# A branch by token count in the layer-0 experts: four column groups for at most 32 tokens, and another order behind the first product

## The chip, the cores and the metric

The kernel runs on one core of a Trainium2 chip. The metric is the device time of one execution in microseconds. Five engines work side by side, each on a queue of its own: TensorE (PE, its weight loads PEld), VectorE (DVE), ScalarE (ACT), GpSimd (POOL) and SyncE (SP, which only issues transfers). They wait for each other by semaphores.

## What is computed

A decoder trunk of two layers over 1024 tokens of width 1024, all in float32. Each layer has a mixer (pooling in layer 0, gated linear attention in layer 1) and a mixture of 64 experts in 8 groups. A token goes to one group and to two experts in it. The part that the change touches:

```python
group_sizes = jnp.bincount(flat_id, length=MOE_EXPERTS).astype(jnp.int32)
gu = lax.ragged_dot(xs, w_in, group_sizes)            # 1024 -> 2 x 384
gate, up = jnp.split(gu, 2, axis=-1)
ys = lax.ragged_dot(jax.nn.silu(gate) * up, w_out, group_sizes)   # 384 -> 1024
ys = ys * weights.reshape(-1)[order][:, None].astype(ys.dtype)
out = jnp.zeros_like(t).at[token_of].add(ys)
```

Each expert has 3 MB of `w_in` and 1.5 MB of `w_out`, and 2048 places for tokens are spread over 64 experts, 32 on average.

## The kernel before

**The experts.** `moe` (L608) walks the 64 experts of a layer in one unrolled loop. The tokens of an expert come in portions of 64, each token as two halves of 512 channels, so that a gathered tile has 128 rows (half, token). For expert e:

- `gather` (L501, POOL) fetches the rows of expert e + 2.
- `expert_first` (L530) multiplies: stationary are 64 tokens by 128 channels (`xT`), moving are 384 columns of `w_in`. The gate goes to one half of a PSUM bank's partitions, the up part to the other, eight steps of 128 channels, 16 `matmul` calls, each two instructions in float32.
- `expert_in` (L508) of expert e + 1 follows on TensorE: four transposes (L512). ScalarE (L520) and VectorE (L522) then scale and shift four pieces each.
- `expert_hidden` (L542): Silu of the gate on ScalarE (L545), times the up part on VectorE (L546).
- `expert_turn` (L548): three transposes (L554) and a copy on ScalarE (L555).
- `expert_last` (L557): the product with `w_out` (L563), weights and gate in `expert_add` (L567), and an accumulating scatter into `x_d` (L569).
- An `If` on the expert's count (L664) does a second portion of up to 64 tokens. The four engines with work in it load the count from `kept` (L619) and branch. TensorE's join waits until the work ahead of it is done.
- `load` issues the three transfers of expert e + 2 (L498, L499) from SyncE into the ring `RING0` of six slots; they stand behind that join, and wait for it.

**Which path.** In layer 1, and for experts 2 to 15 of layer 0, `expert_either` does the whole with one `If`/`Else`. Experts 0, 1 and 16 to 63 of layer 0 go through `expert_out` (L574). Groups are ordered by size, so that early experts have more tokens.

**The filler.** While the experts of layer 0 run, TensorE also computes the input projection of layer 1 in float16 halves. `prep_norm` and `prep_out` prepare a block of 128 tokens (a norm, transposes, two casts on ScalarE at L932); `piece` cuts its product into 49 units: one small product (L944), then 48 pieces of three matmuls (L957), and after each eight of these an eviction on ScalarE (L959) and a transfer to DRAM (L960). `expert_out` runs two units before the turn, two before `expert_last` and four after it, as long as there are units: eight experts have room for 64.

**Order.** TensorE's instructions in the loop stand as the code is written (`manual_schedule`). The other engines' order is made by the scheduler, within the blocks that branches bound. Engines run their queues in order.

Of the kernel before, what the change touches and what calls it, by code (L numbers as in the profile page):

```python
# [11 lines left out]
AF = mybir.ActivationFunctionType  # L12
OP = mybir.AluOpType
AX = mybir.AxisListType
ET = mybir.EngineType
# [4 lines left out]
NE = 64  # L20
# [16 lines left out]
def trunk_kernel(ctx, tc, x_in, c_in, norm_gain, w_mod, b_mod, pool_w, pool_b, pool_scale,  # L37
# [4 lines left out]
    V, S, T, G, SP = nc.vector, nc.scalar, nc.tensor, nc.gpsimd, nc.sync  # L42
# [6 lines left out]
    A = [slots.tile([128, 3072], F32, name=f"slot{i}") for i in range(16)]  # L49
# [7 lines left out]
    def part(slot, kb, n):  # L57
        a = int(kb * 256)
        return A[slot][:, a:a + n]

    def ps():
        return psum.tile([128, 512], F32, name="ps")
# [4 lines left out]
    def cv(n):  # L67
        taken[0] += n
        return kept[:, taken[0] - n:taken[0]]
# [3 lines left out]
    ident = cv(128)  # L73
# [12 lines left out]
    cnt_i = cv(88)[0:1, :].bitcast(I32)  # L86
    wz_, isc_ = cv(128), cv(128)
    wz = wz_.rearrange("p (a b) -> p a b", a=8)
    zst = part(15, 11.25, 32).rearrange("p (b f) -> p b f", b=2)
    ig = cv(128).rearrange("p (a b) -> p a b", a=2).bitcast(I32)  # L90
    isc = isc_.rearrange("p (a b) -> p a b", a=2).bitcast(I32)
    wsl = cv(128).rearrange("p (a b) -> p a b", a=2)
# [1 line left out]
    so = small[:, 58:66].bitcast(I32)  # L94
    G2 = cv(512)
    gs = part(15, 11.5, 40)
    gmax, ginv, gmul, gadd = (gs[:, 8 * i:8 * i + 8] for i in range(4))
    gout = gs[:, 32:33]
    gtmp = gs[:, 33:37]
# [30 lines left out]
    p = ps()  # L130
# [4 lines left out]
    p = ps()  # L135
# [145 lines left out]
    def as16(a):  # L281
        return a.bitcast(BF16)

    def route_consts(area):

        ones_b, trim = as16(area("ones", 64)), as16(area("trim", 64))
        V.memset(ones_b, 1.0)
        V.tensor_tensor(trim, slot_no, pno.to_broadcast([128, 128]), op=OP.is_le)
        V.tensor_scalar(trim, trim, -1.0, None, op0=OP.mult)
        return ones_b, trim  # L290
# [215 lines left out]
    mark = []  # L506
# [23 lines left out]
    def expert_first(i, sl, b=None):  # L530
        xT = part(15, 2 * i, 512).rearrange("p (c g t) -> p c g t", c=4, g=2)
        p1 = ps()
        n = 0
        for g in range(2):
            for cc in range(4):
                W = A[sl[g]].rearrange("p (k u f) -> p k u f", k=4, u=2)[:, cc]
                for u, s in enumerate(sides(i if b is None else b)):
                    T.matmul(p1[s, 0:384], xT[:, cc, g, :], W[:, u], start=n == 0, stop=n == 7)  # L538
                n += 1
        return p1  # L540

    def expert_hidden(b, p1):  # L542
        gate, up = sides(b)
        hh = part(15, 4, 384)[up]
        S.activation(hh, p1[gate, 0:384], AF.Silu)  # L545
        return V.tensor_tensor(hh, hh, p1[up, 0:384], op=OP.mult).ins  # L546

    def expert_turn(b):  # L548
        s = sides(b)[1]
        hh = part(15, 4, 384)[s].rearrange("p (r c) -> p r c", c=3)  # L550
        hT = part(15, 5.5 + 0.75 * b, 192)
        p3 = ps()
        for cc in range(3):
            T.transpose(p3[:, cc * 64:(cc + 1) * 64], hh[:, :, cc], ident[s, s])  # L554
        return S.copy(hT, p3[:, 0:192]).ins  # L555

    def expert_last(b, sl):  # L557
        hT = part(15, 5.5 + 0.75 * b, 192)
        o = A[sl[2]].rearrange("p (k f) -> p k f", k=3)
        p2 = ps()  # L560
        for cc in range(3):
            for g in range(2):
                T.matmul(p2[g * 64:g * 64 + 64, :], hT[:, cc * 64:(cc + 1) * 64],  # L563
                         o[:, cc, g * 512:(g + 1) * 512], start=cc == 0, stop=cc == 2)
        return p2

    def expert_add(l, p2, w, sidx, y):  # L567
        V.scalar_tensor_tensor(XG[y], p2, w, G2, op0=OP.mult, op1=OP.mult)  # L568
        ins = G.indirect_dma_start(out=yv[l], out_offset=bass.IndirectOffsetOnAxis(ap=sidx, axis=0), in_=XG[y],  # L569
                                   in_offset=None, bounds_check=2 * SEQ - 1, oob_is_err=False, compute_op=OP.add).ins  # L570
        while moved:
            tc.add_manual_dep(ins, moved.pop().name, DATA_SYNC, reason="it adds to what they wrote")

    def expert_out(l, i, sl, to, y, between=None, fill=lambda n: None):  # L574
        p1 = expert_first(i, sl)
        if between:
            between()
        fill(2)
        mark[:] = [expert_hidden(i, p1)]
        mark.append(expert_turn(i))  # L580
        fill(2)
        p2 = expert_last(i, sl)
        fill(4)
        expert_add(l, p2, *to, y)

    def expert_either(l, i, sl, to, y, nxt, many, to2, y2, aside):

        def hidden(b, p, n):
            if n:
                return expert_in(l, n[0], n[1], lambda: expert_hidden(b, p))  # L590
            return expert_hidden(b, p)

        p1 = expert_first(i, sl)
        with tc.If(many) as cmp:
            ins = hidden(i, p1, (i, y2))
            aside(ins, expert_turn(i))
            p2 = expert_last(i, sl)
            p1b = expert_first(i, sl, 1 - i)
            expert_add(l, p2, *to, y)
            hidden(1 - i, p1b, nxt)  # L600
            expert_turn(1 - i)
            expert_add(l, expert_last(1 - i, sl), *to2, y2)
        with cmp.Else():
            ins = hidden(i, p1, nxt)
            aside(ins, expert_turn(i))
            expert_add(l, expert_last(i, sl), *to, y)

    def moe(l, ring, mb, ob, load, ng, na, filler=None, before=None, aside=None, after=None):  # L608


        nr = len(ring)
        to = ig if l else isc
        pool_only = (ET.Pool,)

        def slots_at(e):
            return [ring[(3 * e + j) % nr] for j in range(3)]

        def count(e, engines):
            return nc.values_load(cnt_i[0:1, e:e + 1], engines=engines, min_val=0, max_val=SEQ,  # L619
                                  skip_runtime_bounds_check_because=COUNT_REASON)  # L620

        def main(e):
            return mb[e % len(mb)]

        def more(e):
            return ob[e % len(ob)]

        def ahead(e):
            if e < NE:
                with tc.If(count(e, pool_only) > 64):  # L630
                    gather(ig[:, 1, e:e + 1], more(e))

        for e in range(na):
            ahead(e)
        expert_in(l, 0, main(0))
        for e in range(NE):
            i = e % 2
            sl = slots_at(e)

            def between():  # L640
                if e + 1 < NE:
                    expert_in(l, 1 - i, main(e + 1))

            if before:
                before(e)
            if e + ng < NE:
                gather(ig[:, 0, e + ng:e + ng + 1], main(e + ng))
            tos = [(wsl[:, k, e:e + 1], to[:, k, e:e + 1]) for k in range(2)]
            engines = (ET.Pool, ET.Activation, ET.PE, ET.DVE)
            if l or 1 < e < NE // 4 and not units:  # L650
                ahead(e + na)
                expert_either(l, i, sl, tos[0], main(e), (1 - i, main(e + 1)) if e + 1 < NE else None,
                              count(e, engines) > 64, tos[1], more(e), aside or (lambda *marks: None))
                if after:
                    after(e)
            else:
                expert_out(l, i, sl, tos[0], main(e), between,
                           (lambda n: filler(e, n)) if filler else (lambda n: None))
                if aside:
                    aside(*mark)  # L660
                if after:
                    after(e)
                ahead(e + na)
                with tc.If(count(e, engines) > 64):  # L664
                    expert_in(l, i, more(e))
                    expert_out(l, i, sl, tos[1], more(e))
            for s in range(nr + 3 * e, min(nr + 3 * e + 3, 3 * NE)):
                load(s // 3, s % 3, slots_at(s // 3))
# [114 lines left out]
    for half in range(2):  # L783
        s = slice(half * 512, half * 512 + 512)
        S.copy(Q1[:, s], row_psum(pcol[:, 8:16], half, dg[0]))
        p = row_psum(pcol[:, 0:8], half, dg[1])
# [38 lines left out]
    def urgent(r):  # L825
        with tc.high_priority():
            next(r)
            next(r)
        next(r)

    urgent(route(0, 0, NT, area0, route_consts(area0)))
    gather(ig[:, 0, 0:1], 0)
    last = gather(ig[:, 0, 1:2], 1)
# [138 lines left out]
    def filler(e, n):  # L972
        if e < NE - 1:
            run_units(min(n, len(units) - 32) if e > NE - 6 else n)

    def aside(*marks):
        with tc.issue_after(marks[0]), tc.issue_after(marks[1]):
            for step in steps[:4]:
                step()
# [467 lines left out]
```

## Time and profile before

| | us |
|---|---|
| three runs | 2326.62, 2328.43, 2334.72 |
| median | 2328.43 |
| the profiled execution | 2327.7 |
| its span, first to last instruction | 2326.0 |
| TensorE busy in it | 1984.6 (85%) |
| VectorE, ScalarE, GpSimd busy | 718.9, 622.7, 496.9 |
| DMA | 770 MB, mean 331 GB/s |
| experts 16 to 63 of layer 0 | 426 to 1165 |
| layer 1's experts | 1495 to 2295 |

The granted TensorE clock was 0.964 of full speed in the mean. Busy shares of the whole are means over stages with different limits; what the changed stage waits for is read in that stage. In a timeline a row's idle time stands in brackets, with what ended it.

### The profile page before, as it was taken

Reading aid. Unit: us, or ns where it says so; the run is one execution under the profiler, and the core shown is the slowest. Engines: PE = TensorE matmul, PEld = TensorE weight load, DVE = VectorE, ACT = ScalarE, POOL = GpSimd, SP = SyncE. Lnnn points to the kernel's source line nnn. Section 1 sums busy time; section 2 is a strip of 40 time slices with the busy share of each in tenths; the row PEclk is TensorE's granted clock in tenths of the full one; section 3 lists DMA queues with packets and bytes.
Section 4 is the critical chain, followed back from the end, with each engine's and each line's share of the span. In section 5 each row is a group of like instructions: output and inputs, shape, how many; then the busy total and the mean of one; then the engine's idle time right before and its main releaser. Section 6 shows DMA issues by size and latency. Waiting matters only on the chain. (4 is left out here: it accounts for less than half of the span.)

```text
span 2326.0 us, 31279 instructions
## 1 busy us (share of the span) xinstructions
PE 1984.6 (85%) x11195; PEld 945.5 (41%) x11196; DVE 718.9 (31%) x1759; ACT 622.7 (27%) x1418; POOL 496.9 (21%) x422
## 2 busy tenths in 40 slices
PE   7968888899999999999888999888878777778784
PEld 5644333344444444444334565433323332333331
DVE  3454545211121121212147567422211111112122
ACT  4222323322222121212126665221211111112113
POOL 0303222122222221222124110222212212122210
PEclk9979999999999999999988999899999999999997
DMA  9979989998978999989945942699999999999995
GB/s 347 370 297 393 394 292 346 370 342 326 346 286 310 335 363 341 369 313 365 348 132 169 332 165 87 260 395 386 398 382 391 385 380 390 379 391 386 393 382 206
DMA packets 222566, 770.03 MB, mean 331 GB/s; under 512 B 31623, under 2 KB 41261, under 8 KB 201822
## 3 DMA queue, kind: packets, MB, share of 16 engines
q1 hardware_dynamic: 177074, 684.66, 75.4%
q0 software_dynamic: 43856, 77.67, 12.0%
q10 hardware_dynamic: 1372, 4.28, 0.5%
q8 instruction: 154, 2.52, 0.4%
q14 instruction: 110, 0.90, 0.1%
HBM read 735.44 MB, written 69.80 MB: 346 GB/s over the span
## 5 line engine op out<-in xcount | busy, mean ns | idle before, releaser
L538 PE MATMUL ps<-slot,slot 128*64 128x384 f32 x4416 | 757.5, 493 | 94.7 <-DMA slot<-in_moe_w_in_dram 76.2
L538 PEld LDWEIGHTS ps<-slot,slot 128*64 128x64 f32 x4416 | 336.2, 138 | 517.3 <-issue 247.7
L563 PE MATMUL ps<-slot,slot 128*64 128x512 f32 x1656 | 405.4, 626 | 48.0 <-ACT slot L555 46.2
L545 ACT ACTIVATE slot<-ps 64x384 f32<-64x384 f32 x138 | 67.0, 485 | 1265.1 <-PE ps L538 1236.1
L957 PE MATMUL ps<-slot,slot 128*128 128x512 f16 x1152 | 278.8, 388 | 8.6 <-DVEq L1094 5.7
L522 DVE TENSOR_SCALAR slot<-ps,kept 128x64 f32<-128x64 f32 x552 | 151.1, 334 | 339.8 <-PE ps L512 338.5
L546 DVE TENSOR_TENSOR slot<-slot,ps 64x384 f32<-64x384 f32 x138 | 75.8, 549 | 528.4 <-ACT slot L545 527.6
L569 POOL DMA_INDIRECT x_d<-kept x96 | 159.2, 1659 | 362.4 <-DVEq L664 172.1
L563 PEld LDWEIGHTS ps<-slot,slot 128*64 128x64 f32 x1656 | 110.9, 141 | 247.7 <-issue 184.2
L502 POOL DMA_INDIRECT kept<-h_d,kept x96 | 102.1, 1064 | 499.8 <-DMA x_d<-kept 296.6
L520 ACT ACTIVATE slot<-ps,kept 128x64 f32<-128x64 f32 x552 | 178.4, 403 | 59.3 <-PE ps L512 51.2
L568 DVE SCALAR_TENSOR_TENSOR kept<-ps,kept 128x512 f32<-128x512 f32 x96 | 72.0, 750 | 328.8 <-PE ps L563 325.9
L957 PEld LDWEIGHTS <-slot 128*128 128x128 f16 x1152 | 108.2, 100 | 156.3 <-issue 50.1
L554 PE MATMUL ps<-kept,slot 64*128 64x64 f32 x414 | 76.0, 291 | 91.7 <-DVE slot L546 91.4
L554 PEld LDWEIGHTS ps<-kept,slot 64*128 64x128 f32 x414 | 57.8, 202 | 135.7 <-DVE slot L546 102.3
L569 POOL DMA_INDIRECT x_d<-slot,kept x42 | 67.2, 1601 | 159.6 <-DVE slot L568 96.0
L502 POOL DMA_INDIRECT slot<-h_d,kept x42 | 44.2, 1053 | 230.3 <-DMA x_d<-slot,kept 91.5
L1269 PE MATMUL ps<-slot,slot 128*128 128x512 f16 x384 | 85.7, 379 | 1.2 <-DVE slot L1261 0.9
L568 DVE SCALAR_TENSOR_TENSOR slot<-ps,kept 128x512 f32<-128x512 f32 x42 | 31.5, 751 | 122.4 <-PE ps L563 116.5
L512 PE MATMUL ps<-kept 128*128 128x128 f32 x384 | 63.1, 287 | 2.4 <-DMA kept<-h_d,kept 2.4
L512 PEld LDWEIGHTS ps<-kept 128*128 128x128 f32 x384 | 40.4, 141 | 60.5 <-issue 57.1
L1269 PEld LDWEIGHTS <-slot 128*128 128x128 f16 x384 | 37.1, 98 | 46.7 <-issue 2.1
(336 smaller groups left out, 1672.6 us busy)
## 6 DMA issues: line engine op xcount, KB each, us to landing
slot<-in_moe_w_in_dram SPq DMA_DIRECT2D x256, 1536.0 KB, 12.4
slot<-in_moe_w_out_dram SPq DMA_DIRECT2D x128, 1536.0 KB, 13.0
slot<-in_w_mod_dram SPq DMA_DIRECT2D x24, 1536.0 KB, 11.8
slot<-in_gla_w_in_dram SPq DMA_DIRECT2D x8, 1536.0 KB, 8.2
slot<-in_w_mod_dram SPq DMA_DIRECT2D x8, 1152.0 KB, 6.7
h_d<-slot POOLq DMA_DIRECT2D x16, 512.0 KB, 7.1
slot<-in_x_dram SPq DMA_DIRECT2D x8, 512.0 KB, 11.6
slot<-x_d POOLq DMA_DIRECT2D x8, 512.0 KB, 7.2
```

What stands on the lines that cost most here:

```text
L502: return G.indirect_dma_start(out=XG[i], out_offset=None, in_=hv, in_offset=bass.IndirectOffsetOnAxis(ap=idx, axis=0), bounds_check=2 * SE ...
L512: T.transpose(pp[cc % 2][:, cc // 2 * 128:cc // 2 * 128 + 128], XG[g][:, cc * 128:(cc + 1) * 128], ident)
L520: S.activation(xT[:, cc, g, :], pv[:, g, :], AF.Identity, bias=sh, scale=sc)
L522: ins = V.tensor_scalar(xT[:, cc, g, :], pv[:, g, :], sc, sh, op0=OP.mult, op1=OP.add).ins
L538: T.matmul(p1[s, 0:384], xT[:, cc, g, :], W[:, u], start=n == 0, stop=n == 7)
L546: return V.tensor_tensor(hh, hh, p1[up, 0:384], op=OP.mult).ins
L554: T.transpose(p3[:, cc * 64:(cc + 1) * 64], hh[:, :, cc], ident[s, s])
L563: T.matmul(p2[g * 64:g * 64 + 64, :], hT[:, cc * 64:(cc + 1) * 64], o[:, cc, g * 512:(g + 1) * 512], start=cc == 0, stop=cc == 2)
L568: V.scalar_tensor_tensor(XG[y], p2, w, G2, op0=OP.mult, op1=OP.mult)
L569: ins = G.indirect_dma_start(out=yv[l], out_offset=bass.IndirectOffsetOnAxis(ap=sidx, axis=0), in_=XG[y], in_offset=None, bounds_check=2 * ...
L957: T.matmul(p, hP[:, m, kc, :], W[:, n, :], start=kc + i == 0, stop=kc == KC - 1 and i == 2)
L1269: T.matmul(p, oT[:, m, kc, :], woh[kc][:, n, half * 512:(half + 1) * 512], start=kc + i == 0, stop=kc == KC - 1 and i == 2)
```

## The change

Experts 0, 1 and 16 to 63 of layer 0 go through a new function `expert_few` instead of `expert_out`.

- Its first product (`first_of`) stands twice, in the arms of an `If` that TensorE alone takes. With at most 32 tokens, four calls run on 32 columns each: gate and up, and of each the even and the odd steps of 128 channels apart, so that four steps stand where there were eight. With more, it is the product of before.
- ScalarE copies all 128 partitions of the sums to `pc`.
- `turn_of` turns all of `pc`, again in two arms: a product with `pick`, a constant matrix that adds the even and the odd sums, or a transpose. Silu and the product with the up part come behind the turn, on 128 partitions by 192.
- The count for TensorE's new branch is loaded one expert ahead, before the `If(count > 64)`.
- `pick` is filled once; a small buffer (`zst`) moves to make room.

```diff
+    def first_of(few, i, sl):
+        p1 = ps()
...
+        with tc.If(few) as cmp:
+            for n in range(4):
+                for u in range(2):
+                    for odd in range(2):
+                        g, cc = n // 2, n % 2 * 2 + odd
+                        q = 32 * (2 * u + odd)
+                        T.matmul(p1[q:q + 32, 0:384], xT[:, cc, g, 0:32], weights(g, cc, u), start=n == 0, stop=n == 3)
+        with cmp.Else():
+            for n in range(8):
+                for u in range(2):
+                    T.matmul(p1[64 * u:64 * u + 64, 0:384], xT[:, n % 4, n // 4, :], weights(n // 4, n % 4, u),
+                             start=n == 0, stop=n == 7)
+        return p1
+
+    def turn_of(few, b, pc):
...
+        with tc.If(few) as cmp:
+            for cc in range(3):
+                T.matmul(p3[:, cc * 128:(cc + 1) * 128], pv[:, :, cc], pick, start=True, stop=True)
+        with cmp.Else():
+            for cc in range(3):
+                T.transpose(p3[:, cc * 128:(cc + 1) * 128], pv[:, :, cc], ident)
+        p3v = p3[:, 0:384].rearrange("p (c u t) -> p c u t", c=3, u=2)
+        S.activation(hT, p3v[:, :, 0], AF.Silu)
+        return V.tensor_tensor(hT, hT, p3v[:, :, 1], op=OP.mult).ins
+
+    def expert_few(l, i, sl, to, y, few, between, fill):
+        p1 = first_of(few, i, sl)
+        pc = part(15, 4, 384)
+        mark[:] = [S.copy(pc, p1[:, 0:384]).ins]
+        between()
+        fill(2)
+        mark.append(turn_of(few, i, pc))
+        fill(2)
+        p2 = expert_last(i, sl)
+        fill(4)
+        expert_add(l, p2, *to, y)
...
+                few[e] = count(e, (ET.PE,)) <= 32
...
-                expert_out(l, i, sl, tos[0], main(e), between,
-                           (lambda n: filler(e, n)) if filler else (lambda n: None))
+                few_next(e)
+                expert_few(l, i, sl, tos[0], main(e), few.pop(e), between, lambda n: filler(e, n))
...
                 ahead(e + na)
+                few_next(e + 1)
                 with tc.If(count(e, engines) > 64):
```

ScalarE's queue in one ordinary expert of layer 0, before (L545 is the Silu, L520 the shifts of the next expert's tokens, L959 the eviction of the filler, L555 the copy of the turned tile):

```order
L545 ACTIVATE slot_81<-ps 64x384
L520 ACTIVATE slot_81<-ps,kept 128x64 x4
L959 ACTIVATE slot_80<-ps,slot_81 128x512
L555 COPY slot_81<-ps 128x192
L619 TENSOR_LOAD kept
L664 COMPARE_AND_BRANCH
```

The same place now (L521 and L1021 are the shifts and the eviction, L628 the copy of the sums, L622 the Silu; unconditional branches end blocks that only TensorE branches in):

```order
L521 ACTIVATE slot_81<-ps,kept 128x64 x4
L1021 ACTIVATE slot_80<-ps,slot_81 128x512
L628 COPY slot_81<-ps 128x384
L615 UNCONDITIONAL_BRANCH
L622 ACTIVATE slot_81<-ps 128x192
L670 TENSOR_LOAD kept
L722 COMPARE_AND_BRANCH
```

What reads the first product stood ahead of the shifts and the eviction, and now stands behind them. In the expert after a block's norm (seven times) two table loads stand in it, where before there was one ahead of the Silu:

```order
L521 ACT_TABLE_LOAD
L521 ACTIVATE slot_81<-ps,kept 128x64 x4
L1021 ACTIVATE slot_80<-ps,slot_81 128x512
L628 COPY slot_81<-ps 128x384
L615 UNCONDITIONAL_BRANCH
L622 ACT_TABLE_LOAD
L622 ACTIVATE slot_81<-ps 128x192
```

The shifts' wait for TensorE is an instruction of its own in front of the first of these loads. TensorE's queue where one expert ends and the next begins (L722 is the `If(count > 64)` with its arm left out, L596 the new branch, L602 and L606 its arms, L513 the next transposes):

```order
L670 TENSOR_LOAD kept x2
L722 COMPARE_AND_BRANCH
...
L722 UNCONDITIONAL_BRANCH x2
L681 UNCONDITIONAL_BRANCH
L596 COMPARE_AND_BRANCH
L602 MATMUL ps<-slot_75,slot_81 32x384 x8
L602 MATMUL ps<-slot_76,slot_81 32x384 x8
L596 UNCONDITIONAL_BRANCH
L606 MATMUL ps<-slot_75,slot_81 64x384 x8
L606 MATMUL ps<-slot_76,slot_81 64x384 x8
L596 UNCONDITIONAL_BRANCH
```

Both counts are loaded ahead of the join, the new branch stands behind it. The order on GpSimd and SyncE is that of before, but for transfers of the filler that stand a little earlier or later.

## Rows read from the trace of the kernel before

**Rows 1.** Two stretches: us, busy us by engine, TensorE clock, DMA share, GB/s.

```profile
426.00:1165.00 739.00, 691.34 (x3587) 311.43 (x3584) 144.41 (x361) 172.34 (x419) 164.79 (x149) 0.98 0.91 338
1700.00:1800.00 100.00, 77.72 (x395) 31.00 (x391) 17.20 (x43) 14.37 (x42) 21.13 (x16) 0.95 1.02 393
```

**Rows 2.** Timeline, TensorE, expert 33: start, us, line, shape, count, idle before.

```profile
703.29 5.38 PE L538 MATMUL ps<-slot,slot 128*64 128x384 f32 x32 [0.30 <-PEq L664]
708.61 0.66 PE L512 MATMUL ps<-kept 128*128 128x128 f32 x4
709.10 1.46 PE L957 MATMUL ps<-slot,slot 128*128 128x512 f16 x6
710.89 0.53 PE L554 MATMUL ps<-kept,slot 64*128 64x64 f32 x3 [0.33 <-DVE slot L546]
711.35 1.47 PE L957 MATMUL ps<-slot,slot 128*128 128x512 f16 x6
712.75 2.79 PE L563 MATMUL ps<-slot,slot 128*64 128x512 f32 x12
...
718.54 5.38 PE L538 MATMUL ps<-slot,slot 128*64 128x384 f32 x32 [0.30 <-PEq L664]
```

**Rows 3.** Timeline, ScalarE, then VectorE, the same expert.

```profile
708.71 0.49 ACT L545 ACTIVATE slot<-ps 64x384 f32<-64x384 f32 x1 [12.18 <-PE ps L538]
709.36 1.29 ACT L520 ACTIVATE slot<-ps,kept 128x64 f32<-128x64 f32 x4 [0.16 <-PE ps L512]
710.53 0.70 ACT L959 ACTIVATE slot<-ps,slot 128x512 f32<-128x512 f32 x1
711.45 0.32 ACT L555 COPY slot<-ps 128x192 f32<-128x192 f32 x1 [0.22 <-PE ps L554]
...
714.71 1.28 ACT L545 ACT_TABLE_LOAD   x1
...
710.21 0.53 DVE L546 TENSOR_TENSOR slot<-slot,ps 64x384 f32<-64x384 f32 x1
```

**Rows 4.** The prologue, TensorE: the modulation product (L179) and fp32 products of 128x128.

```profile
129.81 1.50 PE L179 MATMUL ps<-slot,slot 128*32 128x384 f32 x16
131.24 1.78 PE L255 MATMUL ps<-slot,slot 128*128 128x72 f32 x14
...
28.47 0.39 PE L767 MATMUL ps<-slot,slot 128*128 128x128 f32 x2
28.70 0.39 PE L770 MATMUL ps<-slot,slot 128*128 128x128 f32 x2
...
L179 PEld LDWEIGHTS ps<-slot,slot x352: 106/110/178, 11.0 to 151.2; 128*32 128x32 f32 x176
L179 PE MATMUL ps<-slot,slot x352: 486/486/850, 11.0 to 151.5; 128*32 128x384 f32 x176
```

**Rows 5.** Line 664 on TensorE's sequencer: ns min/median/max.

```profile
L664 PEldq COMPARE_BRANCH  x51: 70/220/360, 192.0 to 1159.9; - x51
```

**Rows 6.** Timeline, ScalarE: an eviction and what follows it at once.

```profile
547.29 0.69 ACT L959 ACTIVATE slot<-ps,slot 128x512 f32<-128x512 f32 x1 [7.15 <-PE ps L957]
547.88 1.39 ACT L244 ACTIVATE slot<-ps,slot 128x128 f32<-128x128 f32 x3
```

**Rows 7.** Timeline, TensorE, expert 50, without filler.

```profile
968.44 0.52 PE L554 MATMUL ps<-kept,slot 64*128 64x64 f32 x3 [1.76 <-DVE slot L546]
...
969.37 4.14 PE L563 MATMUL ps<-slot,slot 128*64 128x512 f32 x12 [0.41 <-ACT slot L555]
```

**Rows 8.** Timeline, TensorE, expert 30, which begins a block of filler.

```profile
649.59 0.66 PE L512 MATMUL ps<-kept 128*128 128x128 f32 x4
...
652.85 0.61 PE L554 MATMUL ps<-kept,slot 64*128 64x64 f32 x3 [0.26 <-DVE slot L546]
```

**Rows 9.** Scatters, 500:1100, then 1700:2060: count, median us from issue to landing.

```profile
x_d<-kept POOLq DMA_INDIRECT x39, 4.4
x_d<-kept POOLq DMA_INDIRECT x14, 9.1
```

More of the change, by code (lines that the diff above doesn't have):

```diff
@@ L88, in trunk_kernel @@
     wz = wz_.rearrange("p (a b) -> p a b", a=8)
-    zst = part(15, 11.25, 32).rearrange("p (b f) -> p b f", b=2)
+    zst = part(15, 11.6875, 32).rearrange("p (b f) -> p b f", b=2)
     ig = cv(128).rearrange("p (a b) -> p a b", a=2).bitcast(I32)
@@ L96, in trunk_kernel @@
     gs = part(15, 11.5, 40)
+    pick = part(15, 11, 128)
     gmax, ginv, gmul, gadd = (gs[:, 8 * i:8 * i + 8] for i in range(4))
@@ L584, in expert_out, with weights @@
         expert_add(l, p2, *to, y)
+    def first_of(few, i, sl):
+        p1 = ps()
+        xT = part(15, 2 * i, 512).rearrange("p (c g t) -> p c g t", c=4, g=2)
+        def weights(g, cc, u):
+            return A[sl[g]].rearrange("p (k u f) -> p k u f", k=4, u=2)[:, cc, u]
+        with tc.If(few) as cmp:
[12 more added lines that the diff above has]
+    def turn_of(few, b, pc):
+        pv = pc.rearrange("p (r c) -> p r c", c=3)
+        hT = part(15, 5.5 + 0.75 * b, 192).rearrange("p (c t) -> p c t", c=3)
+        p3 = ps()
+        with tc.If(few) as cmp:
[18 more added lines that the diff above has]
+        expert_add(l, p2, *to, y)
     def expert_either(l, i, sl, to, y, nxt, many, to2, y2, aside):
@@ L631, in ahead, with few_next @@
                     gather(ig[:, 1, e:e + 1], more(e))
+        few = {}
+        def few_next(e):
+            if e < NE and e not in few:
+                few[e] = count(e, (ET.PE,)) <= 32
         for e in range(na):
@@ L829, in urgent @@
         next(r)
+    V.memset(pick, 0.0)
+    sides_of = "p (u h t) -> p u h t"
+    V.tensor_tensor(pick.rearrange(sides_of, u=2, h=2)[:, :, 0], ident.rearrange(sides_of, u=2, h=2)[:, :, 0],
+                    ident.rearrange(sides_of, u=2, h=2)[:, :, 1], op=OP.add)
     urgent(route(0, 0, NT, area0, route_consts(area0)))
```

## The prediction

> **What bounds the kernel now.** I read the busy time by stretch first, to see which engine fills the part that is changed. Experts 16 to 63 of layer 0 lie between 426 and 1165 us: TensorE is busy 691 of 739 us, the DMA engines 0.91 of the time, against 1.02 in a stretch of layer 1 that waits for weights [rows 1]. So TensorE sets the pace here, and the DMA engines are not far behind: the same transfers at 1.02 would take 739 x 0.91 / 1.02 = 659 us. Then the timeline of one expert on TensorE and on ScalarE and VectorE, to see the order in it and its gaps [rows 2, 3]. Expert 33 goes from 703.29 to 718.54, 15.25 us: `expert_first` 5.32 until the transposes of the next expert begin (I call that moment E), 0.49 for these, two pieces of filler work, the turn at E + 2.28 with 0.33 idle before it, two pieces, `expert_last`, four pieces, and 0.30 idle at the join of the `If(count > 64)`. TensorE waits for no weights in it.
>
> **What takes the new arm.** The reference's router worked through on its own inputs gives 32 tokens or fewer for 38 of the 50 experts that `expert_few` handles (0, 1 and 16 to 63). Of the 38, 24 have filler around the turn and an eviction of it before (like expert 33), 6 begin a block of filler (18, 24, 30, 36, 43, 59), 8 have little or none (42, 49, 50, 57, 58, 61, 62, 63). Of the 12 others 7 are of the first kind, 51 of the second, and 0, 1, 16, 17 of the last.
>
> **The change, part by part.**
>
> *First product.* Now 32 instructions, two at a time on 64 columns each, 5.32 us. Then 32 instructions, four at a time on 32 columns. The nearest row is the modulation product of the prologue, 16 instructions of 128x32 and 384 elements, four at a time: the next line starts 1.43 us after it [rows 4]. Twice that is 2.86; at the pace of the present pairs, 5.32 / 16 = 0.33 a round, eight rounds are 2.66. I take 2.72, a gain of 2.60 (2.46 to 2.66).
>
> *Branches.* The one at the head of `first_of` comes right behind the join, where TensorE has just run empty, so it is exposed. The present branches take 0.07 to 0.36 us on its sequencer [rows 5]; the few arm stands next and is fallen into, so I take 0.13 for it, and 0.36 for the other, which is jumped to. The jump over the else arm and the second branch run ahead of queued matmuls: nothing, up to 0.3. Loading the count stands ahead of the join behind the filler and `expert_last`: nothing.
>
> *The wait before the turn.* This is where the order matters. The copy of the sums is written first, but stands on ScalarE behind the four shifts of the next expert's tokens and behind the eviction of the filler (order above). Today the Silu stands ahead of them, and the wait is for VectorE. Worked out with today's rows [rows 3, 6]: the shifts start at E + 0.75 (709.36), the eviction at E + 1.92 (710.53), what follows an eviction 0.59 later (547.29 to 547.88), the copy of 384 elements a partition takes the 0.49 of today's Silu of as many, and TensorE starts some 0.1 to 0.15 after what releases it (710.21 + 0.53 to 710.89). So the turn starts at about E + 3.1 instead of E + 2.28: +0.80 (0.66 to 0.95). Without an eviction ahead it starts at E + 2.55.
>
> *The turn.* Three fp32 matmuls of 128x128 are six instructions; in the prologue such a pair follows the last by 0.22 [rows 4], so 0.67 against 0.46 (710.89 to 711.35): +0.20. The else arm transposes and costs as now, or 0.1 less. The Silu (0.32 by the copy of the same size) and the product now come behind the turn: 0.84 + 0.32 + some 0.33 and three hand-overs of 0.05, about 1.65 after its start, while the turn and two pieces of filler keep TensorE for 0.67 + 1.40 = 2.07. Hidden, with 0.4 to spare; the product is half as wide as one of 0.53. Where no filler stands there it shows: 1.65 against 0.93 now (968.44 to 969.37) [rows 7], +0.7; in the else arm, whose transposes are shorter, +0.34. Filling `pick` is two VectorE instructions in the prologue, once: nothing, at most 0.3.
>
> *Table loads.* Behind each of the seven norms of a new block (next experts 17, 21, 27, 34, 42, 50, 58) the Silu's table is loaded 9 us ahead of use today (714.71, 1.28 us) [rows 3]. In the new order the shifts need a table first, and their wait for TensorE stands ahead of that load: the copy is 1.28 later. A second load follows before the Silu, hidden where filler stands, else about 0.3.
>
> *The sum.* Ordinary few experts: -2.60 + 0.13 + 0.80 + 0.20 = -1.47, times 24 = -35.3. Those that begin a block have an fp32 product of 16 instructions before the turn, now at E + 3.26 (649.59 to 652.85) [rows 8]: 18, 43 and 59 have no eviction ahead, and the turn falls to E + 2.85, so -2.68 each; 24, 30 and 36 have two casts between the shifts, about E + 3.7, so -1.82 each; together -13.5. The eight without filler: 49, 57, 61 -1.0 each, 62 and 63 -1.7 each, 42, 50 and 58 have the table load and come to about +0.4 in all; together -6. Table loads at 21, 27 and 34: +3.8. The 12 others: seven at 0.36 + 0.80 - 0.1 = +1.06, the rest +5.4 (a table load in 0 and 17); together +12.8. In all -35.3 - 13.5 - 6 + 3.8 + 12.8 = -38. The stretch would take 701 us with the DMA engines at 0.96; I add 3 us for loads and gathers that come late after the short experts. -35 us from the profiled execution's 2327.7, which lies 0.7 below the median, is **2293**. With every term at its bounds (0.15 and 0.15 on 38, 0.3 for the jump on some, 0 to 10 for the late loads) 2280 to 2306.
>
> **Rivals.** *The DMA engines take the place of TensorE.* The loads for expert e + 2 are released by the join of e, and have one expert's time less its first product. An accumulating scatter lands in 4.4 us in this stretch and in 9.1 in the saturated one [rows 9], and the next gather waits for it. If the engines come to 0.93 with all stalls, the stretch is 739 x 0.91 / 0.93 = 723, 16 us gained: 2312. For it: 0.96 would be needed; against it: layer 1 holds 1.02, though with gathers four ahead where layer 0 has two.
>
> *The copy does not wait.* If ScalarE were done early enough for the turn to follow the filler at E + 1.8, 31 experts would have it 1.3 earlier than forecast, and the table loads (some 8 us) would be hidden: -38 - 40 - 8 = -86. That is more than the 80 that the DMA engines allow at 1.02; at 1.00 they allow 739 - 672 = 67: 2261. Against it: the queue goes in order, and the shifts can't start before E + 0.75.
>
> *Slower: the four column groups do not run side by side here.* The row for it has one stationary operand for all four and fp32 streams from one slot; here the stationary tokens change every round. If the loads of the weights into the array kept it to pairs, 32 instructions stay at 5.32 and the rest is loss: -38 + 38 x 2.60 = +61, 2389. It decides from 2.72 + 38 / 38 = 3.7 us for the product upward. Against it: the modulation product loads its weights for every instruction too, 352 loads for 352 matmuls.
>
> *A drain at each change of column width.* In the rows the burst of 32 columns starts at 129.81 and what follows at 131.24, though the burst lasts to 131.31, so there is no gap to see [rows 4]. If the array did empty there, an instruction's 0.49 less the 0.33 between rounds, 0.16, would be paid twice in 38 experts, 12 us: 2305. [...]
>
> **How the numbers follow.** Forecast 0.64; DMA 0.14, of which 0.05 so strong that nothing measurable is left; no wait 0.08; drain 0.06; slower 0.08. About 7 us, 0.3%, is what a measurement of this kernel can tell from no change. Faster 0.64 + 0.09 + 0.08 + 0.06 = 0.87, same 0.05, slower 0.08. The range of 2262 to 2316 holds the forecast, the drain, most of the DMA case and the weaker part of the case without a wait, and leaves out some 0.17.
>
> **What would show it.** The 32 instructions of 128x32 handing over after 2.7 us; the turn at E + 3.1 with 1.2 to 1.3 us idle before it, put down to ScalarE's copy; about 13.8 us from expert to expert where it was 15.25, and 16.3 in the few of more tokens; the table load between the shifts' wait and the shifts; DMA at 0.95 to 0.97. Wrong would be: a product of over 3.7 us; waits for weights at the head of most experts; a turn that does not wait.

## The result and the profile after

The changed kernel takes 2311.72 us (median of 8 runs, 2305.80 to 2323.23) beside 2326.14 us for the kernel before (8 runs): a ratio of 0.9942, with an interval from 0.9923 to 0.9960. It is faster by 9 to 18 us, about 13.5. The forecast was 35 us: the sign holds, the time lies inside the range, and the gain is 0.4 of what was forecast. The profiled execution has a span of 2309.5 us, 16.5 less than that of before. One execution of those below, of `row_order`, took 2706.15 us at a granted clock of 0.716 and is left out of the times.

The stretch from the first product of expert 16 to that of expert 63, and one expert in it, number 33 as in [rows 2, 3]. First the stretch (us, busy us by engine, TensorE clock, DMA share, GB/s), then TensorE's timeline:

```profile
426.45:1136.17 709.72, 617.12 (x3641) 278.49 (x3638) 135.19 (x359) 175.35 (x424) 161.50 (x147) 0.96 0.93 346
```

```profile
697.65 2.79 PE L602 MATMUL ps<-slot,slot 128*32 128x384 f32 x32 [0.42 <-PEq L722]
700.36 0.66 PE L513 MATMUL ps<-kept 128*128 128x128 f32 x4
700.86 1.46 PE L1019 MATMUL ps<-slot,slot 128*128 128x512 f16 x6
703.41 1.31 PE L617 MATMUL ps<-slot 128*128 128x128 f32 x6 [1.09 <-ACT slot L628]
704.56 1.46 PE L1019 MATMUL ps<-slot,slot 128*128 128x512 f16 x6
705.95 2.80 PE L564 MATMUL ps<-slot,slot 128*64 128x512 f32 x12
708.68 2.76 PE L1019 MATMUL ps<-slot,slot 128*128 128x512 f16 x12
711.87 0.53 PE L602 MATMUL ps<-slot,slot 128*32 128x384 f32 x4 [0.42 <-PEq L722]
```

The same expert on ScalarE:

```profile
701.12 1.29 ACT L521 ACTIVATE slot<-ps,kept 128x64 f32<-128x64 f32 x4 [10.24 <-PE ps L513]
702.29 0.70 ACT L1021 ACTIVATE slot<-ps,slot 128x512 f32<-128x512 f32 x1
702.86 0.50 ACT L628 COPY slot<-ps 128x384 f32<-128x384 f32 x1
704.76 0.33 ACT L622 ACTIVATE slot<-ps 128x192 f32<-128x192 f32 x1 [1.40 <-PE ps L617]
```

Expert 33 takes 14.22 us where it took 15.25. Its first product hands over after 2.71 us instead of 5.32: the four column groups run side by side. The branch adds 0.12 at the join (0.42 for 0.30). The turn starts at E + 3.05, with 1.09 us of waiting for ScalarE's copy, which is third in its queue. And the turn itself takes 1.15 us (703.41 to 704.56) where 0.67 was forecast. That last number is the first hole in the sum.

The second is in the experts without filler. Expert 61 in the kernel before, as a stretch and with its two waits on TensorE, then in the changed kernel as a stretch and on TensorE's timeline:

```profile
1127.06:1138.55 11.49, 9.94 (x55) 4.53 (x55) 1.67 (x6) 2.68 (x7) 0.58 (x1) 1.00 0.96 343
```

```profile
1134.66 0.53 PE L554 MATMUL ps<-kept,slot 64*128 64x64 f32 x3 [0.98 <-DVE slot L546]
1135.59 2.79 PE L563 MATMUL ps<-slot,slot 128*64 128x512 f32 x12 [0.41 <-ACT slot L555]
```

```profile
1110.31:1124.12 13.81, 10.72 (x57) 4.18 (x58) 1.94 (x6) 2.57 (x7) 0.59 (x1) 0.76 0.97 360
```

```profile
1110.31 2.79 PE L602 MATMUL ps<-slot,slot 128*32 128x384 f32 x32 [0.42 <-PEq L722]
1113.03 0.66 PE L513 MATMUL ps<-kept 128*128 128x128 f32 x4
1113.52 0.81 PE L1019 MATMUL ps<-slot,slot 128*128 128x512 f16 x3
1116.08 1.31 PE L617 MATMUL ps<-slot 128*128 128x128 f32 x6 [1.74 <-ACT slot L628]
1118.20 5.39 PE L564 MATMUL ps<-slot,slot 128*64 128x512 f32 x12 [0.81 <-DVE slot L623]
```

Its first product is 2.6 us shorter, its waits are 1.3 longer (1.74 + 0.81 + 0.42 against 0.98 + 0.41 + 0.30), and yet it takes 2.3 us more. The granted clock is 0.76 where it was 1.00: behind two waits the last product runs at a granted clock of 0.50 (from 1117.50 to 1123.70) and takes 5.39 us, where at 1.00 the same twelve instructions take 2.80 (705.95, above). Not every such expert loses its clock: 49 has the same three waits in this profile, keeps 1.00 and takes 11.12 us; in the profile of `row_order`, below, 49 takes 14.58 and 57, which has 13.83 here, takes 10.74. What decides between them is not settled.

By kind of expert, from first product to first product, in us (expert 63 is left out, since its time runs into the next stage; there was a forecast of -1.7 for it):

| experts | forecast | measured |
|---|---|---|
| few tokens, with filler (24, three with a table load) | -31.5 | -19.4 |
| few tokens, beginning a block of filler (6) | -13.5 | -14.7 |
| few tokens, little or no filler (7) | -4.3 | +8.6 |
| more tokens (12) | +12.8 | +14.3 |
| late loads and gathers | +3 | no such wait |
| experts 2 to 15 and the second portion of 31, same code | 0 | -3.2 |

Together that is -14.3; the stages before and behind give the other -2.2 of the -16.5. The -3.2 where nothing was changed shows how far two profiles differ by themselves.

### The profile page after: what moved, and what is told of

The parts are those of the page before. It is cut to its first block, busy times and chain, and to the rows that moved or that the text cites. A ratio compares the mean times of both kernels' runs of the same rounds, so it can differ in the third digit from the quotient of the medians.

```text
span 2309.5 us, 31718 instructions
## 1 busy us (share of the span) xinstructions
PE 1919.8 (83%) x11309; PEld 919.7 (40%) x11310; DVE 710.8 (31%) x1761; ACT 626.4 (27%) x1425; POOL 496.2 (21%) x422
## 3 DMA queue, kind: packets, MB, share of 16 engines
q0 software_dynamic: 43856, 77.67, 12.1%
q8 instruction: 170, 2.79, 0.5%
## 5 line engine op out<-in xcount | busy, mean ns | idle before, releaser
L539 PE MATMUL ps<-slot,slot 128*64 128x384 f32 x2816 | 486.0, 493 | 82.3 <-DMA slot<-in_moe_w_in_dram 79.8
L539 PEld LDWEIGHTS ps<-slot,slot 128*64 128x64 f32 x2816 | 205.1, 138 | 371.0 <-issue 227.5
L521 ACT ACTIVATE slot<-ps,kept 128x64 f32<-128x64 f32 x552 | 178.8, 403 | 436.3 <-PE ps L513 428.2
L546 ACT ACTIVATE slot<-ps 64x384 f32<-64x384 f32 x88 | 42.7, 485 | 782.0 <-PE ps L539 754.5
L564 PEld LDWEIGHTS ps<-slot,slot 128*64 128x64 f32 x1656 | 112.8, 144 | 260.4 <-issue 175.7
L547 DVE TENSOR_TENSOR slot<-slot,ps 64x384 f32<-64x384 f32 x88 | 48.5, 552 | 524.0 <-ACT slot L546 524.0
L1019 PEld LDWEIGHTS <-slot 128*128 128x128 f16 x1152 | 112.5, 101 | 150.2 <-issue 44.0
L602 PE MATMUL ps<-slot,slot 128*32 128x384 f32 x1216 | 106.4, 488 | 16.2 <-PEq L722 14.7
L555 PE MATMUL ps<-kept,slot 64*128 64x64 f32 x264 | 49.0, 292 | 61.9 <-DVE slot L547 61.2
L617 PE MATMUL ps<-slot 128*128 128x128 f32 x228 | 50.5, 361 | 48.6 <-ACT slot L628 48.6
L602 PEld LDWEIGHTS ps<-slot,slot 128*32 128x32 f32 x1216 | 42.8, 109 | 73.9 <-issue 63.6
L606 PE MATMUL ps<-slot,slot 128*64 128x384 f32 x384 | 64.5, 488 | 6.9 <-PEq L722 5.8
L555 PEld LDWEIGHTS ps<-kept,slot 64*128 64x128 f32 x264 | 36.9, 202 | 83.7 <-DVE slot L547 83.4
## 6 DMA issues: line engine op xcount, KB each, us to landing
slot<-in_w_mod_dram SPq DMA_DIRECT2D x24, 1536.0 KB, 10.2
```

The source lines that it names most:

```text
L521: S.activation(xT[:, cc, g, :], pv[:, g, :], AF.Identity, bias=sh, scale=sc)
L602: T.matmul(p1[q:q + 32, 0:384], xT[:, cc, g, 0:32], weights(g, cc, u), start=n == 0, stop=n == 3)
L606: T.matmul(p1[64 * u:64 * u + 64, 0:384], xT[:, n % 4, n // 4, :], weights(n // 4, n % 4, u), start=n == 0, stop=n == 7)
L1019: T.matmul(p, hP[:, m, kc, :], W[:, n, :], start=kc + i == 0, stop=kc == KC - 1 and i == 2)
```

## The experiments

All kernels stand against the kernel before, run on the same chip. Where a single expert is named, it is one that lies between two others with filler, few tokens and no table load, as 33 does.

**Is it the layout of the turn's weights?** The turn loads as its stationary operand every third fp32 element of a row of `pc`. One edit lets ScalarE write the row so that these lie side by side:

```diff
-        pv = pc.rearrange("p (r c) -> p r c", c=3)
+        pv = pc.rearrange("p (c r) -> p r c", c=3)
...
-        mark[:] = [S.copy(pc, p1[:, 0:384]).ins]
+        mark[:] = [S.copy(pc.rearrange("p (c r) -> p c r", c=3), p1[:, 0:384].rearrange("p (r c) -> p c r", c=3)).ins]
```

> The one edit to the changed kernel: ScalarE writes the sums to pc with the index of the column of three outermost, so that each turn matmul loads 128 neighbouring elements of a row as its stationary operand, where it loads every third. Theory: the turn's product takes 1.15 us instead of the forecast 0.67 because loading every third fp32 element is slow (weight loads of 0.26 us started every 0.174 us in the changed kernel; contiguous ones in the prologue 0.19 us every 0.111). Then the product falls to 0.67 to 0.75, 0.40 to 0.48 less in each of 38 experts, and the time from about 2311.7 to about 2295. Rival: a true fp32 product of 128x128 goes at 0.174 an instruction whatever the layout; then the product stays at 1.15 and the time at 2312. Third: ScalarE's copy with a strided read slows by over 0.4 us and gives it back before the turn.

The line's weight loads, in the changed kernel and then in this one (engine, operation, count: ns min/median/max, first and last start, form):

```profile
L617 PEld LDWEIGHTS ps<-slot x228: 251/261/332, 465.3 to 1140.4; 128*128 128x128 f32 x114
```

```profile
L617 PEld LDWEIGHTS ps<-slot x228: 186/192/338, 471.9 to 1137.9; 128*128 128x128 f32 x114
```

The turn of one expert in it:

```profile
695.21 0.94 PE L617 MATMUL ps<-slot 128*128 128x128 f32 x6 [1.10 <-ACT slot L628]
695.98 1.46 PE L1019 MATMUL ps<-slot,slot 128*128 128x512 f16 x6
```

A weight load falls from 0.261 us to 0.192, just what a contiguous one took in the prologue, the turn from 1.15 to 0.77, and the expert from 14.22 to 13.84. So the layout was the cause of 0.38 of the 0.48 that the turn took too long. The other 0.10 is in its first two instructions: they start 0.21 us apart, the others 0.11, and in `copy_front`, below, where TensorE turns without a wait, all start 0.11 apart and the turn takes 0.67. ScalarE's copy takes 0.497 us in both, so the strided read costs it nothing. The time was 2303.94, 0.9886 (0.9826 to 0.9947), too wide to set it apart from the changed kernel; it was run again below.

**Is the wait the queue in front of the copy, and nothing else?** The shifts are issued behind the copy:

```diff
-        between()
+        between(lambda: mark[0])
...
-            def between():
+            def between(first=None):
...
-                    expert_in(l, 1 - i, main(e + 1))
+                    expert_in(l, 1 - i, main(e + 1), first)
```

> The one edit to the changed kernel: the four shifts of the next expert's tokens are issued behind the copy of the sums on ScalarE, so that the copy stands ahead of shifts and eviction. Theory: the 1.09 us that TensorE waits for the copy in each filled expert is the queue in front of the copy alone. Then the turn follows the filler at E + 1.95 with no wait, filled experts of few tokens go from 14.22 to about 13.1 us and those of more from 16.11 to 15.0, the table loads at 21, 27 and 34 are hidden, and experts without filler lose about 1.5 us of waiting; the time comes to about 2262. Rival: the DMA engines, at 0.93 of this stretch now, allow about half of it; then waits for weights appear at the head of the experts, the share comes to 1.0 and the time stays above 2280. Second rival: Silu and product are then late behind the shifts, and the wait moves in front of the last product.

2279.62 us, 0.9792 (0.9744 to 0.9841): a large gain, but the single expert came to 13.63, not 13.1. ScalarE shows why:

```profile
690.71 0.69 ACT L1021 ACTIVATE slot<-ps,slot 128x512 f32<-128x512 f32 x1 [10.83 <-PE ps L1019]
691.30 0.47 ACT L628 COPY slot<-ps 128x384 f32<-128x384 f32 x1
691.65 1.31 ACT L521 ACTIVATE slot<-ps,kept 128x64 f32<-128x64 f32 x4
```

The shifts are behind the copy now, but the eviction is still in front of it, and it waits for pieces of filler until E + 1.3. TensorE waits 0.50 for the copy where it waited 1.09. The second rival shows at 21, 27 and 34: there 0.62 of a wait has moved in front of the last product. The first rival shows at its beginning: the DMA share is 0.97, and TensorE waits for weights in four of the first products, 5.8 us in all, where it was 0.2 in the changed kernel. The pace of the others is not set by the DMA engines yet.

**Are the two independent?** Both edits in one kernel:

> The edits of the two kernels before together. If they are independent the filled experts of few tokens come to about 12.65 us and the time to about 2246. If the DMA engines set the pace they give less than their sum: the stretch of experts 16 to 63 would need the engines at 1.02 of their time, which today's rows of layer 1 show as their limit, and the time would be 2255 to 2265 with waits for weights at the head of most experts.

2269.02 us, 0.9744 (0.9697 to 0.9791). The single expert falls to 13.25: 14.22 - 0.59 - 0.38, so they add up. From the first product of 16 to that of 63 too: 50.2 us less than in the changed kernel, where the two alone give 38.4 and 13.0. The whole is above both expectations, 2246 and 2255 to 2265; the first was worked out from 13.1 us for the expert, where `copy_first` gave 13.63. The waits of the first products for weights come to 6.8 us in this profile.

**The copy in front of everything.** The eviction that falls ahead of the turn is issued behind the copy too:

```diff
-    mark = []
+    mark, front = [], []
...
-        fill(2)
+        front[:] = mark; fill(2); front.clear()
...
-                S.activation(stg[b % 2], p, AF.Copy, scale=gout)
+                with tc.issue_after(front[0]) if front else ExitStack(): S.activation(stg[b % 2], p, AF.Copy, scale=gout)
```

> The kernel `both` with one more edit: an eviction of the filler that falls ahead of the turn is issued behind the copy too (in `both` TensorE still waits 0.50 us before the turn, because the eviction, which ends a group of pieces just then, stands ahead of the copy on ScalarE). Theory: nothing is left in front of the copy, TensorE turns at E + 1.95 without a wait, filled experts of few tokens go from 13.25 to about 12.75 us, some 31 experts by 0.5 each, and the time from 2269 to about 2254. Rival: the DMA engines have no room left for it: then waits for weights stand at the head of the experts (there are a few already, 0.9 to 1.2 us, at 57, 58 and 62) and the time stays at 2262 to 2269.

2247.81 us (2240.10 to 2258.77), 0.9670 (0.9627 to 0.9712). The single expert takes 12.48 us, and the turn waits for nothing:

```profile
671.07 2.79 PE L602 MATMUL ps<-slot,slot 128*32 128x384 f32 x32 [0.42 <-PEq L722]
673.79 0.66 PE L513 MATMUL ps<-kept 128*128 128x128 f32 x4
674.28 1.46 PE L1019 MATMUL ps<-slot,slot 128*128 128x512 f16 x6
675.57 0.83 PE L617 MATMUL ps<-slot 128*128 128x128 f32 x6
676.24 1.46 PE L1019 MATMUL ps<-slot,slot 128*128 128x512 f16 x6
```

It starts at E + 1.78 and lasts 0.67, both as the prediction had them: the 0.67 in its sum, the E + 1.8 in its rival of a copy that does not wait. The stretch from expert 16 to 63, and what ended the idle time of TensorE's matmuls ahead of the first product (us, times):

```profile
424.30:1072.70 648.40, 586.72 (x3641) 262.74 (x3638) 135.00 (x359) 178.03 (x424) 160.97 (x147) 0.98 0.99 377
```

```profile
L602 PE MATMUL ps<-slot,slot x1216: 482/486/844, 452.2 to 1077.1; 128*32 128x384 f32 x174
...
  DMA slot<-in_moe_w_in_dram: 14.6, 10
```

The time is below the 2254 expected, so the rival falls. But the second limit is near: the DMA engines are busy 0.99 of the stretch, and the first products have waited 14.6 us for weights, half of it after short experts (3.4 us at 50, 2.1 at 58 and 62). The longest waits of TensorE here are others, 21.3 us ahead of the last product, for the product on VectorE that stands behind the turn (8.0 in the changed kernel).

**Is it the clock that makes the experts without filler long?** Over experts 57 and 61 of the changed kernel the granted clock was 0.75 and 0.76. In the 12 without filler (0, 1, 16, 17, 42, 49, 50, 57, 58, 61, 62, 63) TensorE does useless products in its waits; nothing reads them:

```diff
+        m = idle_work.get(e, [0]).pop(0) if idle_work.get(e) else 0
+        if m:
+            p = ps()
+            for _ in range(m):
+                T.matmul(p[:, 0:128], ident, ident, start=True, stop=True)
+
+    idle_work = {e: [12 if e in (17, 42, 50, 58) else 7, 4] for e in (0, 1, 16, 17, 42, 49, 50, 57, 58, 61, 62, 63)}
```

> The one edit to the changed kernel: in the 12 experts without filler around the turn (0, 1, 16, 17, 42, 49, 50, 57, 58, 61, 62, 63) TensorE does useless products of 128x128 (7 before the turn, 12 where a table is loaded, 4 behind it) in time in which it waits anyway; nothing reads them. [...] With work in the waits the clock stays up: 57 and 61 go from 13.83 to about 11.2 us, 42 from 16.1 to about 13.5, and the whole is 12 to 18 us shorter, 2294 to 2300, though work was added. Rival: their length is the waits alone; then each stays or gets up to 1 us longer and the time is 2312 to 2318.

Expert 61 on TensorE's timeline:

```profile
1112.37 2.79 PE L602 MATMUL ps<-slot,slot 128*32 128x384 f32 x32 [0.49 <-PEq L722]
...
1116.23 1.72 PE L1041 MATMUL ps<-kept 128*128 128x128 f32 x14
1118.13 1.31 PE L617 MATMUL ps<-slot 128*128 128x128 f32 x6 [0.18 <-ACT slot L628]
1119.28 1.06 PE L1041 MATMUL ps<-kept 128*128 128x128 f32 x8
1120.27 1.94 PE L564 MATMUL ps<-slot,slot 128*64 128x512 f32 x8
```

With 22 instructions more it takes 11.12 us instead of 13.81, at a granted clock of 1.00 instead of 0.76, and 42 takes 13.42 instead of 16.14. The seven experts of few tokens come out 14.8 us shorter together, and 0, 1, 16 and 17 another 8.3. The median, 2303.86 us (2293.39 to 2317.80), 0.9875 (0.9820 to 0.9930), did not settle what of this reaches the end, so this and `row_order` were run again beside the changed kernel, with more rounds.

> The changed kernel as it is, again, so that the two single edits stand beside it on one chip. The time before the first expert differs from execution to execution by up to 25 us (175 to 202 us in the profiles so far, in code that no edit touches), so single times of kernels 10 to 20 us apart overlap. Expected: 2305 to 2320, ratio to the kernel before 0.992 to 0.997.

> The turn's weights contiguous, as before: its experts saved 0.38 us each in the trace, 14.6 us for 38. If that reaches the end, the median lies 10 to 16 us below that of `changed_again`; if what follows (layer 1, or waits for weights) takes it back, under 5.

> The useless products in the 12 experts without filler, as before: those experts were some 23 us shorter in the trace, while the median was only 8 below that of the changed kernel on another chip. If the clock's cost in them is real and typical, the median lies 12 to 22 us below that of `changed_again`; if other experts or stages lose the clock in its place, within 6 us of it.

On one chip: 2321.66, 2308.10 and 2299.57 us, with ratios of 0.9959 (0.9940 to 0.9978), 0.9899 (0.9874 to 0.9924) and 0.9857 (0.9829 to 0.9884). So the layout of the weights is worth 13.6 us and the work in the 12 experts' waits 22 us, each by some 7 either way by the intervals, and both reach the end. In the profiles of the three the stretch from 16 to 63 takes 709.8, 696.2 and 695.7 us. With the useless products the 12 experts (63 left out again) are 23.4 us shorter, but the others of the stretch get longer by 5.6, 21 by 1.4 and 34 by 1.6.

**Does the clock still matter once the copy is in front?** The useless products in the fastest kernel:

> The kernel `copy_front` with the useless products of `idle_work` in the 12 experts without filler. [...] Rival: with the copy in front the waits are short enough by themselves for the clock, or weights are waited for there instead; then it stays within 3 us of `copy_front` or gets longer.

2247.48 us, 0.9650 (0.9608 to 0.9692): the same median as without them, though with intervals this wide 8 us more or less would not show. The author's estimate, with the granted clock of these experts at 1.00, was some 8 us less than the 2254 expected of `copy_front`, about 2246; `idle_work` had come out 7.9 us below the changed kernel. The waits were not short enough by themselves: the granted clock of 42, 50 and 58 is 0.88, 0.81 and 0.80 in `copy_front` and 1.00 here, and these three are shorter by 1.6, 3.2 and 2.8 us. Yet the stretch from 16 to 63 takes 646.5 us for 648.4, since others lose it again, the first product of expert 17 most:

```profile
435.12 8.27 PE L606 MATMUL ps<-slot,slot 128*64 128x384 f32 x32 [5.14 <-ACT ps L986]
```

ScalarE, for which it waits, has itself waited 7.60 us for a transfer of the block whose norm it computes. The first products' waits for weights are shorter than in `copy_front`, 10.2 us for 14.6. So in this profile nearly all of what the clock gives back is lost elsewhere; whether that is so in every execution is not shown.

**The new order alone.** In the changed kernel the branch is set so that no expert takes the new arm:

```diff
-                few[e] = count(e, (ET.PE,)) <= 32
+                few[e] = count(e, (ET.PE,)) > 1000
```

> The changed kernel with the threshold of the new branch set so that no expert takes the arm of few tokens: the new order, the branches and the copy alone, without the four column groups. It computes the same. If the sum is right term by term, every filled expert of few tokens costs what those of many tokens cost, 16.11 us: 14.22 + 2.60 of the first product + 0.36 - 0.12 for the jump - 0.69 - 0.1 for the shorter turn = 16.2, some 1.9 to 2 us more in 38 experts, and the time comes to 2375 to 2390, 50 to 60 us above the kernel before. If the four column groups were worth less than their 2.60 (because what follows is late for another reason), the time stays below 2360.

2380.06 us, 1.0237 (1.0205 to 1.0270): slower than the kernel before, as expected. Expert 33 takes 16.25 us:

```profile
717.66 5.38 PE L606 MATMUL ps<-slot,slot 128*64 128x384 f32 x32 [0.68 <-PEq L722]
722.97 0.66 PE L513 MATMUL ps<-kept 128*128 128x128 f32 x4
723.46 1.46 PE L1019 MATMUL ps<-slot,slot 128*128 128x512 f16 x6
726.01 0.61 PE L620 MATMUL ps<-kept,slot 128*128 128x128 f32 x3 [1.09 <-ACT slot L628]
```

So the change is two large terms that nearly cancel. From the first product of 16 to that of 63, before and then here:

```profile
426.26:1151.85 725.59, 680.40 (x3531) 306.66 (x3527) 142.48 (x359) 171.54 (x417) 161.67 (x147) 0.98 0.91 339
```

```profile
419.66:1205.40 785.74, 686.12 (x3531) 311.15 (x3527) 135.37 (x359) 175.06 (x424) 160.53 (x147) 0.97 0.85 314
```

The kernel before takes 725.6 us, the new order alone 785.7, the changed kernel 709.7: the order, with its branches and its copy, costs 60 us, of which 24 in the nine experts without filler, and the new arms bring 76.

## Why the prediction was right in part

**Right.** The first product: 2.72 forecast, 2.71 measured, so the slow rival (column groups in pairs) falls. So does the drain as a new cost: the rounds of four start 0.32 us apart, the next line 0.46 after the last of them, so 0.14 us is lost there, and behind the product of before it was 0.13. If the array does empty there, it costs no more than that, before and after alike. The branch: 0.13 forecast, 0.12 measured. The jump to the other arm: 0.36 forecast, 0.27 to 0.49 measured. The wait before the turn: E + 3.1 forecast, E + 3.05 measured, behind the shifts and the eviction as read from the order. The table load stands between the shifts' wait and the shifts, as forecast, and the turns at 21, 27 and 34 wait 2.38 us. At 34, on ScalarE and then on TensorE:

```profile
715.32 1.28 ACT L521 ACT_TABLE_LOAD   x1 [7.40 <-PE ps L513]
716.62 1.29 ACT L521 ACTIVATE slot<-ps,kept 128x64 f32<-128x64 f32 x4
717.79 0.70 ACT L1021 ACTIVATE slot<-ps,slot 128x512 f32<-128x512 f32 x1
718.36 0.50 ACT L628 COPY slot<-ps 128x384 f32<-128x384 f32 x1
718.88 1.28 ACT L622 ACT_TABLE_LOAD   x1
...
718.91 1.31 PE L617 MATMUL ps<-slot 128*128 128x128 f32 x6 [2.38 <-ACT slot L628]
```

Silu and product behind the turn are hidden where filler stands. The DMA engines did not take TensorE's place: 0.93 in the stretch, and 0.2 us of waits for weights in the first products.

**Wrong, the turn.** The step that failed is "such a pair follows the last by 0.22, so 0.67": the row was of the same shape and type but read its weights side by side, and the turn reads every third element. Measured 1.15, 0.48 more than forecast; in the 24 experts with filler that is 11.5 of the 12.1 us by which they missed. Put side by side, the weights gave back 0.38 an expert in the trace and 13.6 us at the end. The other 0.10 the row could not show either, since its products do not follow a wait. That the layout is the cause is shown (0.261 us a load against 0.192); by what mechanism it slows the load is not. The trace of before had a sign of it, too: its turn (L554) reads every third element as well, and a weight load of it takes 0.207 us, where one of the transposes of the next expert's tokens (L512), which read theirs side by side, takes 0.140.

```profile
L554 PEld LDWEIGHTS ps<-kept,slot x414: 184/207/217, 190.1 to 2291.5; 64*128 64x128 f32 x138
...
L512 PEld LDWEIGHTS ps<-kept x384: 137/140/225, 181.4 to 2228.9; 128*128 128x128 f32 x192
```

The matmuls in [rows 2] do not show it so plainly: three of these transposes hand over after 0.46 us. In the transposes of the new else arm the loads fall from 0.200 to 0.140 in `row_order`, but the expert by only 0.06 us (16.11 to 16.05).

**Wrong, the experts without filler.** They were forecast at -1.0 to -1.7, or +0.4 for three of them together, with the right waits, but for the turn's 0.48, and durations taken at a granted clock of 1.00. Expert 49, the one of the seven that kept its clock, came out at -0.51: the -1.0 of the forecast and the turn's 0.48. The trace of before showed the risk: a product of 4.14 us at expert 50, in [rows 7], at a granted clock of 0.66 (969.30 to 973.60), where the same twelve instructions take 2.79 in [rows 2], at 1.00. The prediction used that row for the length of a wait and not for its own duration. With shorter work and longer waits in the same expert, the granted clock was between 0.75 and 0.85 in six of the seven. The turn's 0.48 in each makes -0.9 of the -4.3, and the rest of the way to +8.6 goes with the clock: work in the waits gave 14.8 us of these seven back.

**Mis-sized, smaller.** The 3 us for late loads did not come; expert 27 lost 1.0 more than its like, 21, on a slower clock (0.90 for 1.00). Experts that begin a block gained 1.2 more than forecast although the turn's 0.48 is missing in all six, 2.9 us: two errors that cancel.

**The range.** That it held the time is luck: it reached up to 2316 for the case of the DMA engines, 2312, which is not what happened. By its own terms the sum went to 2306 at most. The two bounds of 0.15 on 38 experts fit the product and the wait, whose ranges its text gives; for the turn it gives none, and the error of 0.48 is three times either.

## What to carry to other kernels

A duration taken from a row is safe only for the shape, the type and the layout of that row (here a weight load of one shape and type took 0.192 us side by side and 0.261 at every third element): before the sum, ask in what the operand's step in memory differs. Cutting TensorE's work in a part that already waits can cost more than it saves, as in five of the six experts here whose clock fell (61: 13.81 us for 11.49); read the granted clock of just that part, and durations at both levels (here 2.80 us at 1.00 and 5.39 at 0.50). And where a change moves the first reader of a result behind other work on an in-order engine, price the move alone: here it cost 60 us of the 76 that the new product brought, and putting the copy in front (with the weights in order) gave a kernel at 0.967 of the time before, with the DMA engines at 0.99 of the stretch.

## What was not expected

- Adding work made the kernel faster: 22 useless instructions in expert 61 shortened it from 13.81 to 11.12 us, and all 12 such experts gave 22 us at the end.
- A strided read from PSUM cost ScalarE nothing (0.497 us for 128x384 either way), while a strided weight load cost TensorE 0.069 us on top of 0.192.
- The first expert starts between 174.9 and 201.5 us in the profiles of kernels whose code up to there does nothing different. Why is not settled; it is why two kernels 10 us apart need their experts compared in the traces, or many rounds on one chip.
